# Hybrid encoder trunk on one core: the backward direction's products on off-diagonal quarters, PSUM banks in pairs, a residual subtracted by matmul

## The chip, the cores and the metric

One core of a Trainium2 chip. The metric is the time of one execution in microseconds (us); of several runs the median. The engines are TensorE (PE; its weight loads are listed as PEld), VectorE (DVE), ScalarE (ACT), GpSimd (POOL) and SyncE (SP, which issues the DMAs here).

## The reference

Two layers over 256 positions of width 2048. Each: RMS norm, one input projection, two head groups, gates, one output projection, residual. Group A is a delta-rule recurrence (RWKV-7) with 16 heads of 64, run forward and backward with own decays and rates, the two directions summed. Group B is windowed attention with 16 heads, 4 key heads and a sink. Cut to the recurrence:

```python
def step(S, inp):
    r_t, w_t, k_t, v_t, kk_t, a_t = inp
    s_kk = jnp.einsum('bhvk,bhk->bhv', S, kk_t)
    S = (S * w_t[:, :, None, :]
         - s_kk[..., None] * (a_t * kk_t)[:, :, None, :]
         + v_t[..., None] * k_t[:, :, None, :])
    return S, jnp.einsum('bhvk,bhk->bhv', S, r_t)
...
for d, rev in enumerate((False, True)):
    ...
    y = y + wkv_scan(rh, heads(decay), kd, vh, kk, heads(a), rev)
```

## The kernel before

**Projections.** Each tile of 128 output columns is 16 steps over the contraction (`gemm`), each step three matmuls of 128x128 weights against 256 positions: weights and activations are split into a high and a low part, and high*high, low*high and high*low are summed (L269, L270, L271). ScalarE rounds a streamed weight tile to `hi` (L211), VectorE subtracts to get `lo` (L212). `Stream` holds all projection steps in one line.

**Order of the work.** TensorE's order is the order in which the code is written; the other engines' order is set by a scheduler. `window` goes through 14 slots; in each it lets the generators of the recurrence and the attention take their next step and then runs 4 or 5 projection steps. TensorE has one queue, so a matmul that waits holds up the projections written behind it. The tables STAGE_P, STAGE_I, STAGE_B and ATT say in which slots a generator takes a step.

**The recurrence** works on pairs of heads `p` (8 in each layer; head `h` of the pair is partitions 64h to 64h+63), two directions `d`, and four chunks of 64 positions, in three stages that run one or two windows apart:

- `scan_p` prepares: low-rank decay and rate products into `pz` and `pa` (`low_rank`), decay sums, scaled keys.
- `scan_i` builds per chunk the 64x64 matrices `GE` (L711, L718), transposes (`pt`, copied by L748 and L753), and inverts a triangular matrix by doubling over six LEVELS: `pq` (L791), copied to QF by ScalarE, then two halves of `pd` (L802, L804), written into TC and TT under masks (L805, L806). One step of refinement follows (`pf`, FN, `pn`) and gives VF.
- `scan_b` walks the chunks: RH (L837), the product with VF (L851), the state (L861), scaled by VectorE into the next chunk's operand (L863), and the output `py` (L846, L868). Its last step is `pyt` (L885).

In doubling and recurrence each product is 64 by 64, with head h's operand on partitions 64h and its result on partitions 64h: a diagonal quarter of the array, for both directions.

**PSUM.** Eight banks: two for projections, one each for `py` and `pcc` (all other results of the recurrence), and a ring of four single banks, `ps_w`, which `wbank` hands out in turn. A bank is written again when the readers of its last tile are done.

**Attention** runs late in each layer: `scores` (L917), `flip` (eight transposes L944 into two banks, copied by L947), `values` (L956).

Of the kernel before, what the change touches and what calls it, by code (L numbers as in the profile page):

```python
# [46 lines left out]
STAGE_B = (list(range(1, 14)), [2])  # L47
# [81 lines left out]
def hybrid_trunk_kernel(ctx, tc, xT, wi, wv, wo, par, fing, dup, iup, sink, pos, cst, out):  # L129
# [165 lines left out]
    EYE = cp.tile([128, 64], F16, name="EYE")  # L295
# [6 lines left out]
    def setup():  # L302
        posi = st("t1", [T], I32, bufs=3)
        SY.dma_start(out=posi, in_=pos.to_broadcast([128, T]))
        SY.dma_start(out=FG, in_=fing)
        SY.dma_start(out=SK, in_=sink.to_broadcast([128, DEPTH * 16]))
        cin = st("mv", [C_N - C_KEEP], bufs=3)
        SY.dma_start(out=cin, in_=cst[:, C_KEEP:C_N])
        for l in range(DEPTH):
            s = DP[:, l, 0:NSH]  # L310
            V.tensor_tensor(s, PR[:, l, P_MU0 : P_MU0 + NSH], PR[:, l, P_MU1 : P_MU1 + NSH], op=ALU.add)
            V.tensor_scalar(s, s, -1.0, 1.0, op0=ALU.mult, op1=ALU.add)
            h = DP[:, l, NSH : NSH + 8]
# [36 lines left out]
        V.tensor_copy(band, cin[:, 0:512])  # L350
        V.tensor_copy(EYE, cin[:, 512 + 64 * NL : 576 + 64 * NL])
        yield
# [248 lines left out]
    def layer(l):  # L601
# [24 lines left out]
        def scan_p(p, t):  # L626
# [5 lines left out]
            pz = wbank("pz")  # L632
# [4 lines left out]
            pa = wbank("pa")  # L637
# [65 lines left out]
        def scan_i(p, t):  # L703
            VV, BK, MV = t["v"], t["BK"], t["MV"]
            flat = lambda x: x.rearrange("p d c j -> p (d c) j")
            GE = [st(f"ge{h}", [2, NC, 2, 64], bufs=2) for h in range(2)]
            for d in range(2):
                pgs = [wbank("pg") for _ in range(2)]
                for c in range(NC):
                    for h in range(2):  # L710
                        PE.matmul(  # L711
                            pgs[h][:, c * 128 : (c + 1) * 128],
# [4 lines left out]
                for h in range(2):  # L717
                    V.tensor_tensor(  # L718
                        GE[h][:, d].rearrange("p c s j -> p c (s j)"),
                        pgs[h].rearrange("p (c x) -> p c x", c=NC),  # L720
                        gm[d].unsqueeze(1).to_broadcast([128, NC, 128]),
                        op=ALU.mult,
                    )
# [6 lines left out]
            pts = [wbank("pt") for _ in range(2)]  # L730
# [16 lines left out]
            for h in range(2):  # L747
                A.activation(BT[:, h].rearrange("p d i j -> p (d i j)"), pts[h][:, 0:384], AF.Copy)  # L748
# [21 lines left out]

            TC = st("tv", [2, NC, 64], F16)
# [5 lines left out]
            dch = [(d, c, h) for d in range(2) for c in range(NC) for h in range(2)]  # L777
            hq = lambda x, d, c, h: x[half[h], d, c, :]
            quarter = lambda x, d, c, h: x[half[h], d * T + c * 64 : d * T + (c + 1) * 64]
            for li, b in enumerate(LEVELS):  # L780
# [5 lines left out]
                sub = lambda x, d, c, h, o: pick(x, half[h], d * T + c * 64 + o, [2 * b, 32 // b], [1, b])  # L786
                narrow = lambda x, d, c, h: x[half[h], d * 128 + c * 32 : d * 128 + (c + 1) * 32]
                flat4 = lambda x: x[:, 0:256].rearrange("p (d n b) -> p d n b", d=2, b=b)
                pq = wbank("pq")
                for d, c, h in dch:  # L790
                    PE.matmul(narrow(pq, d, c, h), hq(AB, d, c, h), sub(TC, d, c, h, d * b), start=True, stop=True)  # L791
                if li == 0:
                    V.copy_predicated(t_sub(TC), t_mask, flat4(pq))
                    V.copy_predicated(v_sub(TT), v_mask, v_sub(AB))
                    yield
                    continue

                A.activation(t_sub(QF), flat4(pq), AF.Copy)  # L798
                yield
                pd = wbank("pd")  # L800
                for d, c, h in dch:
                    PE.matmul(narrow(pd, d, c, h), hq(TT, d, c, h), sub(QF, d, c, h, d * b), start=True, stop=True)  # L802
                for d, c, h in dch:
                    PE.matmul(narrow(pd[:, T : 2 * T], d, c, h), hq(QF, d, c, h), sub(TT, d, c, h, (1 - d) * b), start=True, stop=True)  # L804
                V.copy_predicated(t_sub(TC), t_mask, flat4(pd))  # L805
                V.copy_predicated(v_sub(TT), v_mask, flat4(pd[:, T : 2 * T]))  # L806
                yield
            pf = wbank("pf")
            for d, c, h in dch:
                PE.matmul(quarter(pf, d, c, h), hq(AB, d, c, h), hq(TC, d, c, h), start=True, stop=False, skip_group_check=True)  # L810
                PE.matmul(quarter(pf, d, c, h), hq(AL, d, c, h), hq(TC, d, c, h), start=False, stop=True, skip_group_check=True)
            FN = st("q16", [2, NC, 64], F16)
            V.tensor_tensor(FN.rearrange("p d c j -> p (d c j)"), pf, TC.rearrange("p d c j -> p (d c j)"), op=ALU.subtract)
            yield
            pn = wbank("pn")
            for d, c, h in dch:
                PE.matmul(quarter(pn, d, c, h), hq(FN, d, c, h), hq(TT, d, c, h), start=True, stop=True)
# [7 lines left out]
        def scan_b(p, t):  # L825
            GE, MV, BT, SUV, PC, bv = (t[n] for n in ("GE", "MV", "BT", "SUV", "PC", "bv"))

            py = ps_c.tile([128, NC, 64], F32, tag="y", name="py")
            A.activation(py, MSK, AF.Copy, scale=0.0)
            for i in range(NC):  # L830
                ci = [order[d][i] for d in range(2)]
                pc = ps_c.tile([128, 3, 2, 64], F32, tag="c", name="pcc")
                for d in range(2):
                    for h in range(2):

                        r = half[1 - h] if i == 0 else every
                        PE.matmul(pc[half[h], 0, d, :], GE[h][r, d, ci[d], 0, :], SUV[r, d, ci[d], h, :], start=True, stop=True)  # L837
                RH = st("rh", [2, 64], bufs=2)
                A.activation(RH, pc[:, 0], AF.Copy)  # L839
                yield  # L840

                here = lambda h, i=i: pick(SUV, half[h], i * 128 + h * 64, [NC * 128 + (NC - 1 - 2 * i) * 128, 2], [1, 64])
                if i > 0:
                    for d in range(2):
                        for h in range(2):
                            PE.matmul(  # L846
                                py[half[h], ci[d], :], MV[half[h], d, ci[d], 1, :], SUV[half[h], d, ci[d], h, :], start=False, stop=False, skip_group_check=True
                            )
                for d in range(2):
                    for h in range(2):  # L850
                        PE.matmul(pc[half[h], 1, d, :], t["VF"][half[h], d, cs(ci[d])], RH[half[h], d, :], start=True, stop=True)  # L851
                if 0 < i < NC - 1:
                    for h in range(2):
                        PE.matmul(pc[half[h], 2], ident[half[h], half[h]], here(h), start=True, stop=False, skip_group_check=True)  # L854
                for h in range(2):
                    A.activation(here(h), pc[half[h], 1], AF.Copy)  # L856
                yield
                if i < NC - 1:
                    for d in range(2):
                        for h in range(2):  # L860
                            PE.matmul(pc[half[h], 2, d, :], BT[:, h, d, i, :], SUV[:, d, ci[d], h, :], start=(i == 0), stop=True, skip_group_check=True)  # L861
                    for h in range(2):
                        V.tensor_tensor(  # L863
                            here(h, i + 1), pc[half[h], 2], pick(PC, half[h], i, [2 * NC - 1 - 2 * i, 2], [0, 64]), op=ALU.mult
                        )
                for d in range(2):
                    for h in range(2):
                        PE.matmul(py[half[h], ci[d], :], GE[h][:, d, ci[d], 1, :], SUV[:, d, ci[d], h, :], start=False, stop=False, skip_group_check=True)  # L868
# [36 lines left out]
        def scores(j):  # L905
# [3 lines left out]
            pss = [wbank("pscr") for _ in range(2)]  # L909
# [196 lines left out]
```

## Time and profile before

| | |
|---|---|
| median of 3 runs | 1246.04 us (1242.67 to 1246.2) |
| profiled execution, its own time | 1244.23 us |
| its span, first to last instruction | 1242.4 us |
| TensorE busy | 1202.6 us, 97% |
| VectorE busy | 947.5 us, 76% |
| ScalarE busy | 735.6 us, 59% |
| TensorE's granted clock, mean | 0.993 |
| DMA | 134 GB/s mean |

How to read it: "busy" counts an engine while an instruction of it runs. A row of a group names line, engine, operation, output and inputs, shape, count, then busy time, mean of one in ns, and the idle time before with what ended it. "64*64" in a matmul's row is the part of the array in use, rows by columns. A float32 matmul of the code that is not of the rounded kind leaves two records, an fp16 one leaves one. Timeline rows give start and duration in us and join records that follow each other.

### The profile page before, as it was taken

What the parts mean: (1) busy time and instruction counts of PE and PEld (TensorE: products, weight loads), DVE (VectorE), ACT (ScalarE), POOL (GpSimd) and SP (SyncE); (2) the same over time, 40 slices, a digit from 0 to 9 for tenths busy, and PEclk for the clock granted to TensorE, in tenths of its full rate; (3) what the DMA queues carried; (4) which work ended last, traced back from release to release, by engine and by line L of the source; (5) the groups of instructions that cost most, each with busy time, mean ns of one, the idle gap of its engine ahead of it and who ended that gap; (6) DMA issues with size and microseconds to landing.
All of it is one profiled execution on the core that took longest, in us unless ns stands there. A gap on an engine that the chain in (4) does not pass through costs nothing.

```text
span 1242.4 us, 37905 instructions
## 1 busy us (share of the span) xinstructions
PE 1202.6 (97%) x16044; PEld 1113.0 (90%) x16044; DVE 947.5 (76%) x2113; ACT 735.6 (59%) x1838; POOL 18.7 (2%) x23
## 2 busy tenths in 40 slices
PE   7989999999999999999998999999999999999996
PEld 6978999999998889899998888999999989899996
DVE  6988878888886668866666888888887766786654
ACT  6655665666565466655555655665766555675553
POOL 0000000000000000000000000000000000000000
PEclk9999999999999999999999999999999999999998
DMA  6543333223322334367653433323222333435653
GB/s 244 164 141 121 100 103 109 104 93 110 104 97 94 125 112 144 123 225 240 209 186 140 144 104 110 104 99 110 104 93 104 102 112 126 139 131 175 211 191 119
DMA packets 60410, 166.68 MB, mean 134 GB/s; under 512 B 7729, under 2 KB 22737, under 8 KB 60241
## 3 DMA queue, kind: packets, MB, share of 16 engines
q1 hardware_dynamic: 60240, 164.27, 39.0%
q8 instruction: 125, 2.05, 0.6%
q14 instruction: 45, 0.36, 0.1%
HBM read 157.43 MB, written 4.19 MB: 130 GB/s over the span
## 4 chain that ended last, share of the span: by engine, by line
PE 57%; issue 15%; DVE 12%; ACT 9%; DMA 4%; SPq 1%; POOL 0%; DVEq 0%; POOLq 0%; ACTq 0%
PE pm L269 15%; PE pm L271 12%; PE pm L270 12%; DVE lo L212 3%; DMA g<-dup 3%; PE pg L711 2%; ACT hi L211 2%; PE pq L791 2%; PE pd L802 2%; DVE lw L654 1%; PE pcc L837 1%; ACT suv L753 1%; PE pd L804 1%; DMA rrot<-u 1%; PE py L846 1%
## 5 line engine op out<-in xcount | busy, mean ns | idle before, releaser
L269 PE MATMUL pm<-XH,hi 128*128 128x256 f32 x1664 | 496.9, 299 | 10.8 <-ACT XH L174 6.0
L271 PE MATMUL pm<-XH,lo 128*128 128x256 f32 x1664 | 471.3, 283 | 11.5 <-DVE lo L212 11.5
L270 PE MATMUL pm<-XL,hi 128*128 128x256 f32 x1664 | 469.1, 282 | 0.0
L211 ACT ACTIVATE hi<-raw 128x512 fp32r<-128x512 f32 x560 | 327.9, 624 | 205.6 <-PE pm L270 160.4
L212 DVE TENSOR_TENSOR lo<-raw,hi 128x512 fp32r<-128x512 f32 x560 | 369.8, 687 | 99.3 <-ACT hi L211 90.6
L269 PEld LDWEIGHTS pm<-XH,hi 128*128 128x128 f32 x1664 | 315.1, 189 | 36.7 <-issue 13.0
L271 PEld LDWEIGHTS pm<-XH,lo 128*128 128x128 f32 x1664 | 315.7, 190 | 17.0 <-DVE lo L212 16.9
L270 PEld LDWEIGHTS pm<-XL,hi 128*128 128x128 f32 x1664 | 315.8, 190 | 0.7 <-DVE XL L175 0.7
L269 PE MATMUL pm<-MH,hi 128*128 128x256 f32 x512 | 143.9, 281 | 0.7 <-ACT hi L211 0.7
L271 PE MATMUL pm<-MH,lo 128*128 128x256 f32 x512 | 143.7, 281 | 0.4 <-DVE lo L212 0.4
L270 PE MATMUL pm<-ML,hi 128*128 128x256 f32 x512 | 143.6, 280 | 0.0
L269 PEld LDWEIGHTS pm<-MH,hi 128*128 128x128 f32 x512 | 96.4, 188 | 1.7 <-ACT hi L211 1.0
L271 PEld LDWEIGHTS pm<-MH,lo 128*128 128x128 f32 x512 | 96.4, 188 | 0.6 <-DVE lo L212 0.6
L270 PEld LDWEIGHTS pm<-ML,hi 128*128 128x128 f32 x512 | 96.4, 188 | 0.0
L839 ACT ACTIVATE rh<-pcc 128x128 f32<-128x128 f32 x64 | 17.5, 273 | 66.9 <-PE pcc L837 66.5
L856 ACT ACTIVATE suv<-pcc 64x128 f32<-64x128 f32 x128 | 34.1, 266 | 20.9 <-PE pcc L854 19.9
L932 ACT ACTIVATE mv<-mv,mx 128x257 f32<-128x257 f32 x64 | 31.9, 503 | 19.5 <-DVE mx L929 19.4
L791 PE MATMUL pq<-tv,AB 64*64 64x32 f16 x1536 | 40.5, 181 | 1.6 <-DVE tv L805 1.1
L718 DVE TENSOR_TENSOR ge<-pg,C 128x512 f32<-128x512 f32 x64 | 41.2, 683 | 0.7 <-PE pg L711 0.7
L791 PEld LDWEIGHTS <-AB 64*64 64x64 f16 x1536 | 33.7, 109 | 7.7 <-issue 1.1
L711 PE MATMUL pg<-mv,bk 64*128 64x128 f32 x512 | 37.2, 285 | 0.0
L798 ACT ACTIVATE QF<-pq 128x256 f16<-128x256 f32 x80 | 30.8, 385 | 9.5 <-PE pq L791 6.6
(230 smaller groups left out, 1866.7 us busy)
## 6 DMA issues: line engine op xcount, KB each, us to landing
raw<-wi SPq DMA_DIRECT2D x207, 512.0 KB
raw<-wo SPq DMA_DIRECT2D x64, 512.0 KB
raw<-wv SPq DMA_DIRECT2D x8, 512.0 KB
rrot<-u SPq DMA_DIRECT2D x80, 32.0 KB
vg<-xT SPq DMA_DIRECT2D x16, 128.0 KB
xd<-vg SPq DMA_DIRECT2D x16, 128.0 KB
vg<-xd SPq DMA_DIRECT2D x16, 128.0 KB
g<-dup SPq DMA_DIRECT2D x16, 97.0 KB
```

The source lines that it names most:

```text
L211: A.activation(hi[:, q], raw[:, q], AF.Copy)
L212: V.tensor_tensor(lo[:, q], raw[:, q], hi[:, q].bitcast(F32), op=ALU.subtract)
L269: PE.matmul(pm, wh, rh[:, kk, :], start=(kk == 0), stop=False)
L270: PE.matmul(pm, wh, rl[:, kk, :], start=False, stop=False)
L271: PE.matmul(pm, wl, rh[:, kk, :], start=False, stop=(kk == 15))
L711: PE.matmul(pgs[h][:, c * 128 : (c + 1) * 128], BK[half[h], d, c, 1 - h : 3 - h, :].rearrange("p s j -> p (s j)"), MV[half[h], d, c].rearr ...
L718: V.tensor_tensor(GE[h][:, d].rearrange("p c s j -> p c (s j)"), pgs[h].rearrange("p (c x) -> p c x", c=NC), gm[d].unsqueeze(1).to_broadca ...
L791: PE.matmul(narrow(pq, d, c, h), hq(AB, d, c, h), sub(TC, d, c, h, d * b), start=True, stop=True)
L798: A.activation(t_sub(QF), flat4(pq), AF.Copy)
L802: PE.matmul(narrow(pd, d, c, h), hq(TT, d, c, h), sub(QF, d, c, h, d * b), start=True, stop=True)
L856: A.activation(here(h), pc[half[h], 1], AF.Copy)
L932: A.activation(Sc[:, h, q, 0:257], Sc[:, h, q, 0:257], AF.Exp, scale=0.125, bias=mx[:, q : q + 1], accum_out=den[:, q : q + 1])
```

## The change

**Quarters.** In doubling and in the recurrence, the backward direction's products (d = 1) of one half read partitions of head h and write those of the other head, h^1: `half[h ^ d]`. So four products, two heads by two directions, use the four quarters. QF, TT and VF of the backward direction stand on swapped halves, which the second half of `pd` and `pn` swap back: those stay on the diagonal. TT's first level, a plain masked copy of AB before, needs the swapped copy of AB for the backward direction; two matmuls with EYE make it, and a second masked copy takes it in.

**Banks in pairs.** `ps_w` becomes two buffers of two banks (`wpair`), since the two directions write different banks. `wbank` hands out the first bank of a pair. `pz` and `pa` share one pair `pza`; the two banks of `pg`, of `pt`, of the attention's `pscr` and `ppt` become one pair each. GE of both heads becomes one tile, filled by one VectorE instruction per direction, and `pt` is copied by one ScalarE instruction. `py` and the state share a tile `pyc` of two banks; the product with VF goes to a pair `pu`. The clearing of `py` by ScalarE falls away, a start flag takes its place. The step with `pyt` moves from slot 2 to 3.

**Residual.** FN was `pf` minus TC on VectorE. Now a product with NEYE (minus the identity) is added in `pf`, and ScalarE copies the sum.

```diff
-STAGE_B = (list(range(1, 14)), [2])
+STAGE_B = (list(range(1, 14)), [3])
...
-    ps_w = pool("ps_w", 4, space=PSUM)
+    ps_w = pool("ps_w", 2, space=PSUM)
+    def wpair(name):
+        return ps_w.tile([128, 2, 512], F32, tag="w", name=name)
     def wbank(name):
-        return ps_w.tile([128, 512], F32, tag="w", name=name)
+        return wpair(name)[:, 0]
...
-            pz = wbank("pz")
+            pza = wpair("pza")
+            pz, pa = pza[:, 0], pza[:, 1]
...
             A.activation(LW, pz, AF.Tanh, scale=0.5)
-            pa = wbank("pa")
...
-            dch = [(d, c, h) for d in range(2) for c in range(NC) for h in range(2)]
+            dch = [(d, c, h) for c in range(NC) for d in range(2) for h in range(2)]
+            hx = lambda x, d, c, h: x[half[h ^ d], d, c, :]
...
-                    PE.matmul(narrow(pq, d, c, h), hq(AB, d, c, h), sub(TC, d, c, h, d * b), start=True, stop=True)
+                    PE.matmul(narrow(pq[:, d], h ^ d, c), hq(AB, d, c, h), sub(TC, h, d, c, d * b), start=True, stop=True)
...
-                    PE.matmul(narrow(pd, d, c, h), hq(TT, d, c, h), sub(QF, d, c, h, d * b), start=True, stop=True)
+                    PE.matmul(narrow(pd[:, d], h, c), hx(TT, d, c, h), sub(QF, h ^ d, d, c, d * b), start=True, stop=True)
...
-                    PE.matmul(narrow(pd[:, T : 2 * T], d, c, h), hq(QF, d, c, h), sub(TT, d, c, h, (1 - d) * b), start=True, stop=True)
+                    PE.matmul(narrow(pd[:, 0, 128 + d * 128 :], h ^ d, c), hx(QF, d, c, h), sub(TT, h ^ d, d, c, (1 - d) * b), start=True, stop=True)
...
+                    PE.matmul(
+                        pf[half[h ^ d], d, 0:T], NEYE[half[h]], TC[half[h], d].rearrange("p c j -> p (c j)"), start=True, stop=False, skip_group_check=True
+                    )
...
-            V.tensor_tensor(FN.rearrange("p d c j -> p (d c j)"), pf, TC.rearrange("p d c j -> p (d c j)"), op=ALU.subtract)
+            A.activation(FN.rearrange("p d c j -> p d (c j)"), pf[:, :, 0:T], AF.Copy)
...
-            py = ps_c.tile([128, NC, 64], F32, tag="y", name="py")
-            A.activation(py, MSK, AF.Copy, scale=0.0)
+            pyc = ps_c.tile([128, 2, 512], F32, tag="yc", name="pyc")
+            pS = pyc[:, 0, 0:128].rearrange("p (d j) -> p d j", d=2)
+            py = pyc[:, 1, 0:256].rearrange("p (c j) -> p c j", j=64)
...
-                        PE.matmul(pc[half[h], 1, d, :], t["VF"][half[h], d, cs(ci[d])], RH[half[h], d, :], start=True, stop=True)
+                        x = half[h ^ d]
+                        PE.matmul(pu[half[h], d, 0:64], t["VF"][x, d, cs(ci[d])], RH[x, d, :], start=True, stop=True)
...
-                            here(h, i + 1), pc[half[h], 2], pick(PC, half[h], i, [2 * NC - 1 - 2 * i, 2], [0, 64]), op=ALU.mult
+                            here(h, i + 1), pS[half[h]], pick(PC, half[h], i, [2 * NC - 1 - 2 * i, 2], [0, 64]), op=ALU.mult
...
+            pp2 = wpair("ppt")
             for h in range(2):
-                ppt = wbank("ppt")
+                ppt = pp2[:, h]
```

Three places in TensorE's order, with the engines that a row waits for in brackets (Activation is ScalarE, DVE is VectorE).

TensorE, a step of `scan_b` in a steady window: state (L861, later L891), then output (L868, later L898). Before:

```order
L270 MATMUL pm<-XL,hi 128x256
L271 MATMUL pm<-XH,lo 128x256
L861 MATMUL pcc<-suv,bt 64x64 [waits Activation_49]
L861 MATMUL pcc<-suv,bt 64x64 x3
L868 MATMUL py<-suv,ge_3544 64x64
L868 MATMUL py<-suv,ge_3545 64x64
```

The output followed the state with no wait of its own. After:

```order
L275 MATMUL pm<-XH,lo 128x256
L891 MATMUL pyc<-suv,bt 64x64 [waits Activation_49] x2
L891 MATMUL pyc<-suv,bt 64x64 x2
L898 MATMUL pyc<-suv,ge 64x64 [waits DVE_49]
L898 MATMUL pyc<-suv,ge 64x64 x3
```

Now the output's first matmul waits for VectorE; the count it waits for is that of the second L893 (L863 before), the product that reads this step's state.

TensorE, the low-rank products of `scan_p`. Before:

```order
L618 MATMUL pz<-acc,duh 128x256
L619 MATMUL pz<-TW,du 128x256
L617 MATMUL pa<-XA,iuh 128x256 [waits Activation_49]
L618 MATMUL pa<-rrot,iuh 128x256
L619 MATMUL pa<-XA,iu 128x256
```

The wait was for the bank's last reader, a copy of `pt` from two slots ahead (L753). After:

```order
L623 MATMUL pza<-acc,duh 128x256
L624 MATMUL pza<-TW,du 128x256
L622 MATMUL pza<-XA,iuh 128x256 [waits Activation_49]
L623 MATMUL pza<-rrot,iuh 128x256
L624 MATMUL pza<-XA,iu 128x256
```

The row looks alike, but the count is now that of L642 (L636 before), the tanh that reads the first half, which the matmul just ahead has only finished.

TensorE, the transposes of `flip` in the attention. Before:

```order
L271 MATMUL pm<-XH,lo 128x256
L944 MATMUL ppt<-C,mv 128x128 [waits PE_49]
L944 MATMUL ppt<-C,mv 128x128 x3
L944 MATMUL ppt<-C,mv 128x128 [waits DVE_49]
L944 MATMUL ppt<-C,mv 128x128 x3
```

The second head's wait was for the older reader of another bank. After:

```order
L979 MATMUL ppt<-C,mv 128x128 [waits DVE_49]
L979 MATMUL ppt<-C,mv 128x128 x3
L979 MATMUL ppt<-C,mv 128x128 [waits Activation_49]
L979 MATMUL ppt<-C,mv 128x128 x3
L273 MATMUL pm<-XH,hi 128x256
```

The second head's transposes wait for L982 (L947 before), the copy of the first head's.

More of the change, by code (lines that the diff above doesn't have):

```diff
@@ L294, in hybrid_trunk_kernel @@
     MSK = cp.tile([128, NC, 64], F16, name="MSK")
-    EYE = cp.tile([128, 64], F16, name="EYE")
+    EYE, NEYE = (cp.tile([128, 64], F16, name=n) for n in ("EYE", "NEYE"))
     band = cp.tile([128, 512], BF16, name="band")
@@ L351, in setup @@
         V.tensor_copy(EYE, cin[:, 512 + 64 * NL : 576 + 64 * NL])
+        V.tensor_scalar(NEYE, EYE, -1.0, None, op0=ALU.mult)
         yield
@@ L728, in scan_i @@
             yield
-            pts = [wbank("pt") for _ in range(2)]
+            pt2 = wpair("pt")
+            pts = [pt2[:, h] for h in range(2)]
             for b in range(2):
@@ L792, in scan_i @@
[L792 to L794 removed]
+                sub = lambda x, r, d, c, o: pick(x, half[r], d * T + c * 64 + o, [2 * b, 32 // b], [1, b])
+                narrow = lambda o, r, c: o[half[r], c * 32 : (c + 1) * 32]
+                flat4 = lambda x: x.rearrange("p d (n b) -> p d n b", b=b)
+                pq = wpair("pq")
+                if li == 0:
+                    for d, c, h in dch:
+                        PE.matmul(narrow(pq[:, 0, d * 128 :], h, c), hq(AB, d, c, h), sub(TC, h, d, c, d * b), start=True, stop=True)
+                    for h in range(2):
+                        PE.matmul(pq[half[1 - h], 1, 0:T], EYE[half[h]], AB[half[h], 1].rearrange("p c j -> p (c j)"), start=True, stop=True)
+                    V.copy_predicated(t_sub(TC), t_mask, flat4(pq[:, 0, 0:256].rearrange("p (d x) -> p d x", d=2)))
+                    one = lambda x, o: pick(x, every, o, [2 * b, 128 // b], [1, b])
+                    V.copy_predicated(one(TT, b), v_mask[:, 0], one(AB, b))
+                    V.copy_predicated(one(TT, T), v_mask[:, 1], one(pq[:, 1], 0))
@@ L867, in scan_b @@
                     for h in range(2):
-                        PE.matmul(py[half[h], ci[d], :], GE[h][:, d, ci[d], 1, :], SUV[:, d, ci[d], h, :], start=False, stop=False, skip_group_check=True)
+                        PE.matmul(
+                            py[half[h], ci[d], :], GE[h][:, d, ci[d], 1, :], SUV[:, d, ci[d], h, :],
+                            start=(i == 0 and d == 0), stop=(i >= NC // 2), skip_group_check=True,
+                        )
                 if i < NC - 1:
```

72 lines of the change are left out of this document (37 added, 35 removed).

## The prediction

> **What bounds the kernel now.** I read the page's first two parts, then the table by stretches of the span, then who waited for whom, then the groups by line, and last the timeline of one steady stretch.
>
> ```profile
> span 1242.4 us, 37905 instructions
> PE 1202.6 (97%) x16044; PEld 1113.0 (90%) x16044; DVE 947.5 (76%) x2113; ACT 735.6 (59%) x1838; POOL 18.7 (2%) x23
> 750.00:850.00 100.00, 99.89 (x1727) 90.36 (x1724) 86.09 (x180) 62.21 (x165) 2.01 (x2) 1.00 0.30 101
> PE pm L271 <- DVE lo L212: 11.9, 18, 1.6
> PE pcc L837 <- DVE suv L863: 1.7, 2, 1.4
> ```
>
> In the steady stretch TensorE is busy for 99.89 of 100 us at full clock, VectorE for 86, ScalarE for 62. Over the whole span TensorE waited 11.9 us for its largest releaser and 1.7 us for the recurrence. So TensorE is the bound. Work taken from it shortens the span, and a wait put into its queue, which holds the projections too, lengthens it almost one for one.
>
> **What the quarters bring.** The bursts that the change spreads, by groups and in the timeline (start us, us, engine, line, operation; "x16" are sixteen records that follow each other):
>
> ```profile
> L791 PE MATMUL pq<-tv,AB 64*64 64x32 f16 x1536 | 40.5, 181 | 1.6 <-DVE tv L805 1.1
> L802 PE MATMUL pd<-QF,tt 64*64 64x32 f16 x1280 | 33.4, 181 | 0.0
> L804 PE MATMUL pd<-tt,QF 64*64 64x32 f16 x1280 | 32.4, 179 | 0.0
> L851 PE MATMUL pcc<-rh,vf 64*64 64x64 f32 x512 | 25.9, 220 | 0.0
> L810 PE MATMUL pf<-tv,AB 64*64 64x64 f16 x256 | 10.6, 195 | 0.6 <-DVE tv L805 0.6
> ```
>
> ```profile
> 258.79 0.68 PE L885 MATMUL pyt<-C,ysq 64*64 64x64 f32 x16
> 259.31 0.33 PE L851 MATMUL pcc<-rh,vf 64*64 64x64 f32 x5
> 259.43 0.27 PE L734 MATMUL pt<-C,vg 64*64 64x64 f32 x1
> 259.43 0.22 PE L851 MATMUL pcc<-rh,vf 64*64 64x64 f32 x1
> 259.44 0.27 PE L734 MATMUL pt<-C,vg 64*64 64x64 f32 x1
> 259.48 0.22 PE L851 MATMUL pcc<-rh,vf 64*64 64x64 f32 x2
> 259.54 0.40 PE L734 MATMUL pt<-C,vg 64*64 64x64 f32 x14
> 262.61 0.42 PE L791 MATMUL pq<-tv,AB 64*64 64x32 f16 x16
> 266.36 0.28 PE L619 MATMUL pz<-TW,du 97*128 97x256 f32 x1
> 266.47 0.28 PE L617 MATMUL pa<-XA,iuh 96*128 96x256 f32 x1
> ```
>
> L885 and L851 use the two diagonal quarters, L734 already all four. Without the last record's own 0.22 us, L885 starts one matmul per (0.68-0.22)/15 = 31 ns and L734 one per (0.40-0.22)/13 = 14 ns, in the same shape: four quarters run at twice the pace of two. The fp16 burst L791 takes (0.42-0.18)/15 = 16 ns per matmul on two quarters, so 8 on four. Per burst of 16 that saves 0.128 us.
>
> - Levels 2 to 6, pq: 5 bursts for 16 head pairs, 80 x 0.128 = 10.2 us. Level 1 stays on the diagonal; its two new products with EYE use the other quarters, 0 to 0.22 us each head pair; I take 0, since L734 ran beside L851.
> - pd, first half (L802): 80 x 0.128 = 10.2 us. The second half (L804) lands on diagonal quarters for both directions: 0. pn likewise: 0.
> - pf: 32 matmuls at 8 ns less, 0.256 us, against four new 256-column products with NEYE, 0.11 us side by side and 0.44 us in a row (the pace of the two 256-column rows at 266.36 and 266.47). I take side by side: 16 x 0.146 = 2.3 us.
> - The products of the recurrence with VF (L851): 8 records at 31 ns, half of it saved, 0.124 us x 64 = 7.9 us; the first RH of each head pair likewise, 16 x 0.124 = 2.0 us.
>
> Sum 32.6 us at most. The lower end is a start pace that can't go under L734's 14 ns: then the fp16 bursts gain 2 ns a matmul, 160 bursts x 16 x 2 ns = 5.1 us, and the sum is 15 us. I take 32.6, because the rows at 259.43 and 259.44 show three starts within 10 ns.
>
> One rule of the Trainium skill speaks against this, in "TensorE: Matmul & The Clock Gate", under "What overlaps and what doesn't": matmuls start and end strictly in program order. The new order within a burst meets diagonal quarters as A, B, B, A, and by that rule L804's 80 bursts and pn's 16 would, by an estimate, lose some 4 us. The trace disagrees: two L734 records start at 259.43 and 259.44, ahead of the last two of L851 at 259.48, which stand before them in the program.
>
> **What the shared tiles cost.** Two things that had tiles of their own now share one, and the program then makes TensorE wait for the reader of the one before it writes the other. The trace shows what such a wait within a burst does:
>
> ```profile
> 390.18 0.28 PE L734 MATMUL pt<-C,vg 64*64 64x64 f32 x2
> 390.89 0.45 PE L734 MATMUL pt<-C,vg 64*64 64x64 f32 x14 [0.43 <-DVE ge L718]
> 391.80 0.39 PE L269 MATMUL pm<-XH,hi 128*128 128x256 f32 x1
> ```
>
> The third record starts 0.71 us after the first; the projections behind it come only after the burst. There are four such places; these rows, and the two at 266.36 and 266.47 above, size them:
>
> ```profile
> 131.70 0.40 PE L868 MATMUL py<-suv,ge 128*64 128x64 f32 x8
> 131.99 0.59 DVE L863 TENSOR_TENSOR suv<-pcc,pc 64x128 f32<-64x128 f32 x2 [1.24 <-PE pcc L861]
> 262.28 0.40 PE L868 MATMUL py<-suv,ge 128*64 128x64 f32 x8
> 263.34 0.58 DVE L863 TENSOR_TENSOR suv<-pcc,pc 64x128 f32<-64x128 f32 x2
> 267.53 0.60 ACT L636 ACTIVATE lw<-pz 128x512 f32<-128x512 f32 x1
> 272.27 0.40 PE L868 MATMUL py<-suv,ge 128*64 128x64 f32 x8
> 273.50 0.69 DVE L212 TENSOR_TENSOR lo<-raw,hi 128x512 fp32r<-128x512 f32 x1
> 274.11 0.58 DVE L863 TENSOR_TENSOR suv<-pcc,pc 64x128 f32<-64x128 f32 x2
> 281.72 0.40 PE L868 MATMUL py<-suv,ge 128*64 128x64 f32 x8
> 282.79 0.58 DVE L863 TENSOR_TENSOR suv<-pcc,pc 64x128 f32<-64x128 f32 x2
> 264.15 0.77 ACT L753 ACTIVATE suv<-pt 64x256 f32<-64x256 f32 x2
> 472.69 1.04 PE L944 MATMUL ppt<-C,mv 128*128 128x128 f32 x8
> 474.48 0.58 ACT L947 ACTIVATE pp<-ppt 128x512 f32<-128x512 f32 x1
> ```
>
> (a) py behind the state, 48 times. Today L868 follows L861 at once, and VectorE's two products L863 come when they come. In the changed program the first py product waits for the second of them. Floor: at 131.99 VectorE stood idle for L861 and still ended at 132.58, 0.88 us after L868 began. Ceiling: VectorE as late as in the steady stretch, 263.92-262.28 = 1.64, 274.69-272.27 = 2.42 and 283.37-281.72 = 1.65 us for the three steps. I take the floor for the first and third, since VectorE catches up while TensorE stands. The second hangs on a chain of VectorE's own: from L636's end (268.13) to L863's end it took 6.56 us, and the new order puts one more L212 (0.69 us) ahead, 7.25. TensorE needs 272.27-266.47 = 5.80 us from pa to L868, less 0.25 saved: 5.55. So 1.7 us. Twelve head pairs at 0.88+1.7+0.88 = 41.5 us; the last two of each layer have no preparation beside them, 4 x 2.64 = 10.6. Sum 52.1 us.
>
> (b) pa behind L636, 16 times: pz and pa share a pair. Floor: last pz matmul 266.36+0.28, L636's 0.60, against pa's start at 266.47: 0.77 us. Ceiling: L636 as late as now, 268.13-266.47 = 1.66 us. I take 1.2, the middle, since ScalarE keeps the copies of RH and QF ahead of it: 19.2 us.
>
> (c) pq of level 1 behind the copies of pt, 12 times: with two buffers it takes the pair that pt leaves. Today L753 ends at 264.92, 2.31 us after pq began. Now pyt's burst (258.79 to 259.31, 0.52 us) stands between, and the pause of (a), 0.88 us: 0 to 0.9 us remain. I take 0.2, since two ScalarE copies that went ahead now go behind: 2.4 us.
>
> (d) The second head's transposes of the attention behind the first head's copy, 16 times. L944's eight start at 0.11 us each, so the second four are due at 473.13. Floor: 473.02+0.27+0.58 = 473.87, 0.74 us. Ceiling: the copy's end at 475.06, 1.93 us. I take 1.1, nearer the floor, since ScalarE is the least loaded of the three: 17.6 us.
>
> **The rest.** L718's two products over 512 columns become one over both banks, FN's subtraction goes from VectorE to ScalarE, pt's two copies become one, the clearing of py falls away, TT of level 1 is copied in two parts: neither engine is the bound, and the next reader stands a slot away. If that cover were gone, FN would cost its one pass of 0.6 us (as L636) x 16 = 10 us. pyt one slot later is waited for by nobody. Attention's other tiles are released before they are taken again. No DMA and no row of SP or POOL moves.
>
> **Sum.** -32.6 + 52.1 + 19.2 + 2.4 + 17.6 = +58.7 us. The profiled execution took 1244.2 us, so 1302.9; the median of the runs shown lies 1.8 us higher: 1305. With every wait at its floor the costs are 42.2+12.3+0+11.8 = 66.3 us and the time is 1280; with every wait at its ceiling 91.4+26.6+10.8+30.9 = 159.7 us, 1373.
>
> **The rivals.**
>
> - Faster, 1213 us. The waits cost nothing, because the releaser is done when TensorE comes, or TensorE runs the projections past the waiting row, as it ran L734 past L851. The gain decides when the 92 waits average under 32.6/92 = 0.35 us. Against it: the two L863 alone take 0.58, and at 390.89 TensorE did not run past.
> - The queues do not catch up: up to 1373, all ceilings. For it: VectorE's 86%. Against it: each pause of TensorE lowers that share.
> - The quarters don't do what they should, start pace 14 ns: gain 15 instead of 32.6, 1322 us. It lies within the range.
>
> **Chances.** Waits between floors and ceilings, 1272 to 1350: 0.80, with the 1322 of the weak quarters in it. Ceilings beyond 1350: 0.07. A little above before, 1250 to 1272, some waits below their floors: 0.02. Within 0.3%, which is about what the runs can tell from no change: 0.03. Faster: 0.08. So 0.08, 0.03, 0.89, and the range is 1272 to 1350.
>
> **What would show it.** Right: new rows among TensorE's waits, py on the state's product (48 times, 40 to 60 us with the drain), pza on lw, ppt on pp; TensorE's idle time up from 40 to some 120 us; pq and L819's bursts of 16 lasting 0.30 us instead of 0.42. VectorE's busy share falls under 73%. Wrong: bursts that keep 0.42 us, or py rows that follow the state's rows with no idle time, or a lower granted clock.

## The result, and the profile after

The changed kernel takes 1358.79 us (median of 4 runs, 1355.82 to 1360.66) against 1246.12 us (1242.67 to 1247.05): ratio 1.0907, 95% interval 1.0877 to 1.0938, 112.7 us slower. I had forecast 1305 us, in a range of 1272 to 1350: the sign was right, the size 54 us too small. The profiled execution spans 1354.0 us, 111.6 more than before.

The first lines of the page of after (span; busy time of each engine):

```profile
span 1354.0 us, 38019 instructions
PE 1209.1 (89%) x16140; PEld 1107.6 (82%) x16140; DVE 946.0 (70%) x2082; ACT 742.4 (55%) x1822; POOL 18.9 (1%) x23
```

Span minus busy time was 39.8 us before and is 144.9 us now: TensorE stands 105.1 us longer. Its busy time has not fallen either, though its bursts got shorter. For whom TensorE waits in after (engine, tile and line; releaser; us, times, longest):

```profile
PE pyc L898 <- DVE suv L893: 53.8, 48, 2.9
PE pza L622 <- ACT lw L642: 28.6, 16, 6.5
PE ppt L979 <- ACT pp L982: 17.2, 16, 1.5
PE pq L813 <- DVE tv L806: 7.7, 13, 0.7
PE pm L275 <- DVE lo L216: 7.0, 9, 1.3
PE pm L273 <- ACT hi L215: 3.7, 2, 2.4
PE pq L803 <- ACT suv L759: 1.2, 2, 0.6
```

The first three rows are the forecast's (a), (b) and (d), 99.6 us; before, none of them stood in this list. The fourth is new and was not forecast. The last is (c). (Rows that the changed waits do not concern are left out.) One pause of kind (a), in the timeline of a steady stretch:

```profile
258.89 0.45 PE L891 MATMUL pyc<-suv,bt 128*64 128x64 f32 x8
259.19 0.69 DVE L216 TENSOR_TENSOR lo<-raw,hi 128x512 fp32r<-128x512 f32 x1 [0.73 <-ACT hi L215]
259.80 0.58 DVE L893 TENSOR_TENSOR suv<-pyc,pc 64x128 f32<-64x128 f32 x2
260.44 0.45 PE L898 MATMUL pyc<-suv,ge 128*64 128x64 f32 x8 [1.10 <-DVE suv L893]
```

L891 and L898 use 128 rows of the array, so they are not among the products that moved to other quarters. L898 follows L891 after 1.55 us; before, the distance (L861 to L868) was 0.28 us on average. VectorE was busy with a weight tile (L216) when the state came, then made its two products, and only then could py start.

In the single bursts the quarters do what was forecast. Two more pieces of the timeline of after:

```profile
254.01 0.30 PE L819 MATMUL pd<-QF,tt 64*64 64x32 f16 x16
254.16 0.41 PE L821 MATMUL pd<-tt,QF 64*64 64x32 f16 x16
...
256.28 0.27 PE L881 MATMUL pu<-rh,vf 64*64 64x64 f32 x2
256.32 0.23 PE L873 MATMUL pyc<-suv,mv 64*64 64x64 f32 x2
...
256.45 0.20 PE L813 MATMUL pq<-tv,AB 64*64 64x32 f16 x2
256.50 0.28 PE L884 MATMUL pyc<-suv,C 64*64 64x128 f32 x2
```

L819 on four quarters takes 0.30 us for 16 records (L802 before: 0.42), L821 on two still 0.41. L881 starts ahead of the last of L873, which stands before it in the program; L813 ahead of L884. My reading, which no run isolates, is that such a row is held up only by its own quarter. It holds for rows with no wait for another engine: at 260.44 the wait for VectorE held up all that stood behind it.

**The granted clock.** Its mean fell from 0.993 to 0.973: 76.1 us of after are at half clock, in 16 stretches (the last at the end of the program; the expectations below count 15), against 19.9 us in 3 before. (These times run to the end of the clock's record, 2.0 us behind the last instruction.) Windows of 3.4 us in after (start, end and length; busy us of PE, PEld, DVE, ACT, POOL; granted clock; DMA's share and GB/s):

```profile
61.40:64.80 3.40, 1.42 (x12) 1.21 (x11) 2.12 (x4) 1.47 (x3) 0.00 (x0) 1.00 0.32 74
64.80:68.20 3.40, 0.00 (x0) 0.00 (x0) 0.00 (x0) 0.39 (x2) 0.00 (x0) 0.50 0.81 286
68.20:71.60 3.40, 2.84 (x13) 2.84 (x14) 2.43 (x5) 2.16 (x6) 0.00 (x0) 0.50 0.03 11
71.60:75.00 3.40, 3.40 (x18) 3.40 (x18) 1.35 (x3) 1.65 (x4) 0.00 (x0) 0.50 0.00 0
...
382.25:385.65 3.40, 2.17 (x35) 1.65 (x33) 3.21 (x8) 2.67 (x7) 0.00 (x0) 1.00 0.47 146
385.65:389.07 3.42, 3.35 (x15) 3.36 (x16) 2.38 (x5) 1.68 (x5) 0.00 (x0) 0.50 0.53 167
389.07:392.48 3.41, 3.41 (x72) 3.22 (x70) 3.23 (x8) 2.51 (x8) 0.00 (x0) 1.00 0.00 0
```

After a window in which TensorE worked 1.42 or 2.17 us comes one at half clock. It takes no long standstill: in the second case pauses of together 1.2 us were enough. To price it I took, for all matmuls that started at half clock, the distance to the next start, and subtracted the mean distance of the same pair of lines at full clock (distances of 0.6 us or more left out). That gives 24.7 us in after, 3.3 before: 21.4 us of the 111.6 are the clock's. I use this measure, "the clock's excess", below.

### The profile page after: what moved, and what is told of

It is laid out like the page before. It is cut to its first block, busy times and chain, and to the rows that moved or that the text cites. A ratio compares the mean times of both kernels' runs of the same rounds, so it can differ in the third digit from the quotient of the medians.

```text
span 1354.0 us, 38019 instructions
## 1 busy us (share of the span) xinstructions
PE 1209.1 (89%) x16140; PEld 1107.6 (82%) x16140; DVE 946.0 (70%) x2082; ACT 742.4 (55%) x1822; POOL 18.9 (1%) x23
## 5 line engine op out<-in xcount | busy, mean ns | idle before, releaser
L216 DVE TENSOR_TENSOR lo<-raw,hi 128x512 fp32r<-128x512 f32 x560 | 369.5, 687 | 118.7 <-ACT hi L215 109.0
L273 PEld LDWEIGHTS pm<-XH,hi 128*128 128x128 f32 x1664 | 322.1, 194 | 35.1 <-issue 13.0
L275 PEld LDWEIGHTS pm<-XH,lo 128*128 128x128 f32 x1664 | 322.2, 194 | 8.4 <-DVE lo L216 8.4
L274 PEld LDWEIGHTS pm<-XL,hi 128*128 128x128 f32 x1664 | 322.6, 194 | 0.7 <-DVE XL L179 0.7
L898 PE MATMUL pyc<-suv,ge 128*64 128x64 f32 x512 | 29.0, 234 | 53.8 <-DVE suv L893 53.8
L898 PEld LDWEIGHTS pyc<-suv,ge 128*64 128x64 f32 x512 | 20.1, 136 | 62.5 <-DVE suv L893 60.4
L868 ACT ACTIVATE rh<-pyc 128x128 f32<-128x128 f32 x64 | 17.3, 270 | 85.2 <-PE pyc L866 85.2
L886 ACT ACTIVATE suv<-pu 64x128 f32<-64x128 f32 x128 | 34.3, 268 | 27.9 <-PE pq L813 19.1
L399 DVE TENSOR_TENSOR u<-pm,rb 128x256 f32<-128x256 f32 x52 | 21.2, 410 | 34.4 <-PE pm L275 32.5
L724 DVE TENSOR_TENSOR ge<-pg,C 128x1024 f32<-128x1024 f32 x32 | 39.1, 1221 | 3.6 <-PE pg L718 3.6
L822 DVE CAST_PREDICATED tv<-LV,pd 128x256 f16<-128x256 uint8 x80 | 34.4, 430 | 9.7 <-PE pd L821 9.6
```

The costliest lines, as they stand in the source:

```text
L216: V.tensor_tensor(lo[:, q], raw[:, q], hi[:, q].bitcast(F32), op=ALU.subtract)
L273: PE.matmul(pm, wh, rh[:, kk, :], start=(kk == 0), stop=False)
L274: PE.matmul(pm, wh, rl[:, kk, :], start=False, stop=False)
L275: PE.matmul(pm, wl, rh[:, kk, :], start=False, stop=(kk == 15))
L399: V.tensor_tensor(u, pm, L.norm.rb, op=ALU.mult)
L724: V.tensor_tensor(GEd(d), pg.rearrange("p h (c x) -> p h c x", c=NC), gm[d].unsqueeze(1).unsqueeze(1).to_broadcast([128, 2, NC, 128]), op= ...
```

## The experiments

Theory: each shared tile costs its pause, one for one. Rivals: a pause taken away comes back at the next wait; the clock is a cost of its own.

**e1: py and state in tiles of their own.**

```diff
-            pyc = ps_c.tile([128, 2, 512], F32, tag="yc", name="pyc")
+            pcc = ps_c.tile([128, 512], F32, tag="c", name="pcc")
+            pyt = ps_c.tile([128, 512], F32, tag="y", name="py")
```

The first RH of each pair is then copied in two instructions instead of one.

> The changed kernel, with py and the state in two tiles of one bank each instead of one tile of two banks, so that py's products no longer wait for VectorE's product of the state. Theory (each wait of a shared tile costs its own drain, and nothing takes its place): the 48 pauses at L898, 53.8 us of idle time and 62 us from start to start, go; 1359 - 62 = 1297 us, with 1285 to 1308 as the clock comes back or not. Rival 1 (the wait moves: TensorE only comes sooner to the next product that needs VectorE or ScalarE, RH on suv or pq on tv): over 1330 us, with new rows of 20 us or more among TensorE's waits. Rival 2 (the clock gate: a window of 3.4 us in which TensorE is busy for half or less is followed by one at half clock): half-clock stretches fall from 15 to 8 or fewer, and the gain is 5 to 10 us more than the pauses alone, 1287 to 1292.

Measured: 1291.67 us, 67.1 less. No row of py's wait is left, and the row of L813, 7.7 us in after, has gone with it, so that wait too hangs on the shared tile. Half-clock time is 51 us in 10 stretches, the clock's excess 14.3. But (c), now uncovered, grew from 1.2 to

```profile
PE pq L803 <- ACT suv L759: 11.5, 12, 1.5
```

So 67 us are one tile's sharing with its after-effects: 62.0 us of pauses (taken from start to start, below), 7.7 of L813 and 10.4 of the clock, less 10.3 for (c), would make 69.8. (c) was small only because (a) covered it, as the prediction's working for (c) had it.

**e2: both low-rank products ahead of the tanh.**

```diff
-            LW = st("lw", [2 * T])
-            A.activation(LW, pz, AF.Tanh, scale=0.5)
             for d in range(2):
                 low_rank(pa[...
+            LW = st("lw", [2 * T])
+            A.activation(LW, pz, AF.Tanh, scale=0.5)
```

> The changed kernel, with both low-rank products (pz and pa) written before ScalarE's tanh of the first, so that pa does not wait for it. Theory (a wait costs its own drain): 37 us from start to start go, or 25 if the two long ones of 6.5 us at the layers' starts are ScalarE's lateness and come back at the next product; 1322 to 1334 us. Rival (the wait moves to the next reader of ScalarE's work): 1345 us or more.

Measured: 1343.65 us, only 15.1 less, though the row of pza, 28.6 us, is gone. The waits of e2 say where it went; in after these rows had 53.8, 7.0 and 3.7:

```profile
PE pyc L898 <- DVE suv L893: 58.7, 48, 2.8
PE pm L275 <- DVE lo L216: 10.6, 13, 1.6
PE pm L273 <- ACT hi L215: 6.9, 4, 2.0
```

The other engines had used the pause to catch up. The time lies between the two ranges, 1.4 us short of the rival's, and the rival's reason holds: of 28.6 us of idle time about half comes back, at these rows.

**e3: the flip's eight transposes ahead of both copies** (the loop over the copies is split off).

> The changed kernel, with all eight transposes of the attention's flip before the two copies. Theory: 16 pauses of 1.1 to 1.3 us go, 17 to 21 us; 1338 to 1342 us. Rival (values waits for the copies instead, or VectorE's scores): 1352 or more.

Measured: 1338.27 us, 20.5 less, as expected by the theory.

**e4: all three.**

> The three edits together. Theory (the three waits add up and the quarters' gain of 22 to 33 us remains): 1246 - 22 to 1246 - 33 us, so 1213 to 1224; with some 9 us of new wait at level 1 of the doubling left, 1220 to 1233. TensorE's busy share is back at 96% or more. Rival 1 (part of the waits moves): 1250 to 1300. Rival 2 (the clock gate is a cost of its own, set by windows with TensorE at half busy or less): half-clock stretches are back at 3 to 5, against 15, and the gain over the changed kernel exceeds the sum of the three single edits or of their idle times (53.8 + 28.6 + 17.2 = 99.6 us) by 10 us or more.

Measured: 1247.09 us, ratio to before 1.0007 (0.9996 to 1.0017): the three waits are worth 111.7 us together, the whole loss; alone they gave 67.1 + 15.1 + 20.5 = 102.7. Half-clock time is 26.8 us in 5 stretches. But the quarters' gain is not there, and the time is in no range of the expectation; of the second rival the stretches came, and the gain stands near its mark of 10 us: 9.0 over the sum of the single ones, 12.1 over the idle times. Page and waits of e4:

```profile
PE 1180.6 (95%) x16140; PEld 1088.7 (88%) x16140; DVE 937.3 (75%) x2082; ACT 738.4 (59%) x1838; POOL 19.0 (2%) x23
...
PE pq L803 <- ACT suv L759: 10.0, 11, 1.5
```

TensorE works 22.0 us less than before and stands 23.6 us longer, 10.0 of it in (c); the rest is spread over rows that grew by 3.5 us or less.

**e5: e4, and two of the four copies of pt on VectorE**, against (c).

> The three edits together, and two of the four copies of pt into suv on VectorE instead of ScalarE. With the three waits gone, TensorE's row pq of level 1 waits 10.0 us in 11 times for ScalarE's last copy of pt, term (c) of the prediction, which had been sized at 2.4 us because the pauses of (a) covered it. Theory: that wait is what hides the quarters' gain; it goes, and the time is 1247 - 8 to 1247 - 11, so 1236 to 1239 us, 0.8% under the kernel before. Rival (the wait moves: VectorE, 75% busy, gets later, and TensorE waits for lo or for the state's product instead): 1243 to 1250.

Measured: 1245.28 us, 0.9995 (0.9984 to 1.0006): no change.

```profile
PE 1180.6 (95%) x16140; PEld 1089.9 (88%) x16140; DVE 951.2 (76%) x2114; ACT 729.1 (59%) x1806; POOL 19.0 (2%) x23
...
PE pq L805 <- DVE suv L762: 14.0, 12, 1.7
...
261.17 0.85 DVE L762 COPY suv<-pt 64x256 f32<-64x256 f32 x2 [0.92 <-ACT suv L764]
```

The copies read the two banks of one pair and write one tile, and VectorE's wait for ScalarE's to end (the last row, of the timeline). So TensorE's wait changed engines. The time is in the rival's range, but not for its reason: the wait for lo stayed (11.1 us, 11.4 in e4).

**e6: e5 with all products on the diagonal** (`h ^ d` becomes `h`).

> The kernel of the previous run, with the backward direction's products put back on the diagonal quarters (h ^ d becomes h everywhere; banks, tiles and order unchanged). It prices the quarters alone. Theory by the rows of the three edits together (pq -6.7 us, both halves of pd -4.4, pf -1.9, the recurrence's products with VF and MV -4.4 against before): slower by 15 to 20 us. The prediction's own sum: slower by 32.6. Rival (TensorE's start pace binds and four quarters bring little): slower by 5 or less.

Measured: 1267.67 us, 1.0177 (1.0158 to 1.0196), 22.4 us over e5, between the theory's 15 to 20 and the prediction's 32.6.

```profile
PE 1212.0 (95%) x16140; PEld 1121.1 (88%) x16140; DVE 955.9 (75%) x2114; ACT 729.4 (57%) x1806; POOL 19.0 (1%) x23
```

TensorE's busy time differs by 31.4 us; the spans differ by 25.1, since e5 stands 6.3 us longer. The rest of the change, without quarters and without the three waits (but with e5's copies), costs 21.9 us (e6 against the runs of before beside it, 1245.76): 12.8 are (c), and pq and pf, with the products with EYE and NEYE in them, take 6.0 us more from start to start. So in e5 a gain of 22.4 us and a cost of 21.9 cancel. That they are so nearly equal is chance.

**e7: e5 with the residual subtracted on VectorE** (the backward direction then takes the other half's TC; only the time is read).

> The kernel of the run before last, with the residual's subtraction back on VectorE: no products with NEYE, FN is pf minus TC on VectorE. Theory (four 256-column products side by side cost TensorE 2.1 us in all, and VectorE has slack there): 2 us faster, from 3 faster to no change. Rival (pn then waits for VectorE): 4 to 10 us slower.

Measured: 1250.27 us, 1.0036 (1.0023 to 1.0048), 5.0 us over e5. The rival's time holds, but the wait is at another row than it said (pg, not pn); so in e5 the move to TensorE is worth 5 us:

```profile
PE pg L718 <- DVE ge L724: 8.1, 14, 0.7
```

**e8 and e12: the pause filled.** Four products of the identity with itself into pu's bank (e8), then two into unused columns of the projections' bank (e12):

```diff
+                    if S.cur is not None:
+                        for _ in range(2):
+                            PE.matmul(S.cur[:, T : T + 128], ident, ident, start=True, stop=True, skip_group_check=True)
```

> The changed kernel, with four products of the identity with itself (128x128, float32, into a part of pu's bank that nobody reads) between the state's products and the waiting py, 48 times: TensorE works through most of the pause that it otherwise stands idle in. They add no result. Theory of the clock gate (in the trace of the changed kernel all 19 windows of 3.4 us with TensorE busy for half or less but one are followed by a window at half clock, none of those at 0.67 or more; 15 such stretches, about 16 us of longer projections): half-clock stretches fall to 8 or fewer and the kernel gets faster, by 5 to 12 us, though it does more work: 1347 to 1354 us. Rival (the pauses cost their idle time and nothing else): 1359 to 1364, no change or a little slower, where fillers outlast a pause.

> The changed kernel, with two products of the identity with itself (128x128, float32, 0.37 us each as the earlier run with four of them showed) in the pause between state and py, 48 times, now into a part of the projections' bank that nobody reads, so that no buffer is held longer. They add no result. Theory of the clock gate (a window of 3.4 us with TensorE busy for half or less is followed by one at half clock): they lift the share of windows that hold two pauses; half-clock stretches fall from 15 to 8 or fewer, and the kernel gets faster by 4 to 10 us, 1349 to 1355. Rival (pauses cost only their idle time): 1358 to 1364.

Measured: e8 1373.65 us, outside both ranges. It tells nothing on the clock: pu's buffer was held longer, and a new wait came up,

```profile
PE pyt L920 <- ACT suv L759: 24.8, 12, 2.2
```

e12, whose fillers also disturb the projections' sums: 1350.22 us, 8.6 less than the changed kernel, with work added. That is in the theory's range and below the rival's 1358. Half-clock time fell from 76.1 to 60.6 us, less than expected (11 stretches, not 8); the clock's excess fell by 5.7 us.

**e9 and e10: e4, with three or two of slot 3's projection steps run ahead of level 1 of the doubling.**

> The three edits together, and in slot 3 of a window three of the five projection steps run ahead of level 1 of the doubling instead of behind it, so that TensorE has work while ScalarE copies pt. Theory (the wait for the copies of pt, 10.0 us in 11 times with the three edits alone, is what stands between that kernel and a gain): 1247 - 8 to 1247 - 10, 1237 to 1239 us. Rival (level 2 then comes too soon after level 1, and TensorE waits for VectorE's copy into TC instead): 1243 to 1249.

> As the run before, with two projection steps ahead of level 1 and three behind. Theory: two steps last 0.72 us and the wait was 0.91 us on average, so some 2 us of it stay; 1238 to 1241 us. Rival (the wait for VectorE's copy into TC takes over): 1243 to 1249.

Measured: 1276.54 us (1.0238, 1.0215 to 1.0262) and 1261.39 us (1.0118, 1.0103 to 1.0133). The rival's wait came in both, but the times are far above its 1249 us. (c) is all but gone, and in its place stands, in e9,

```profile
PE pq L816 <- DVE tv L809: 21.3, 16, 1.4
```

Close behind it pza waits for the same copies (3.2 us). TensorE stands 5.4 us longer than in e4, but the profiled span grew by 26.1: the clock's excess rose from 6.4 to 23.4 us (half-clock time from 26.8 to 70.7). No expectation had that.

**e11: the changed kernel, with three projection steps run between state and py; e14: this and e2's edit.**

> The changed kernel, shared tiles and all, with three of the slot's projection steps run between the state's products and the waiting py. The wait stays in the program, the work that the pause keeps from running goes into it. Theory (a pause costs what TensorE has to stand for, not the wait itself): three steps take 1.08 us of the 1.3 us, so 53.8 us of idle time fall to some 12; 1300 to 1315 us, near the kernel with separate tiles (1292). Rival (VectorE gets later by the steps' own demands, and the wait stays as long): over 1330.

> The kernel with the covered pause (1333 us), and both low-rank products written before ScalarE's tanh. There, level 2 of the doubling waits 15.3 us in 14 times for VectorE and pza 29 us in 26 times right behind it, in the same slot: two pauses within one window of 3.4 us, and 108 us at half clock, the most of all kernels, though its idle time is 103 us against 145 of the changed kernel. Theory of the clock gate (each us at half clock adds 0.58 us to TensorE's busy time, as the kernels so far line up): with one of the two pauses gone, half-clock time falls to some 50 us, and the time falls by 29 + 0.58 * 58 = 62 us, to 1265 to 1280. Rival (only idle time counts): by 29 us or less, to 1304 or more.

Measured: e11 1332.76 us, e14 1305.56: both in the range of the rival, not of the theory. Waits of e11, then the busy time in e14:

```profile
PE pza L627 <- ACT lw L647: 26.3, 16, 6.5
PE pq L818 <- DVE tv L811: 15.3, 14, 1.7
PE pyc L904 <- DVE suv L898: 3.9, 5, 1.5
```

```profile
span 1300.9 us, 37994 instructions
PE 1209.3 (93%) x16140; PEld 1101.8 (85%) x16140; DVE 943.8 (73%) x2082; ACT 741.1 (57%) x1822; POOL 19.0 (1%) x23
```

In e11 the wait of (a) is covered, 3.9 us of 53.8 are left, against the rival's reason; yet only 26 us come back: the second row doubled and stands in the same slot as the first, two pauses in one window, and half-clock time is 108 us (excess 33.6), the most of all kernels. With the first row gone, in e14, half-clock time is 50.9 us (excess 16.4), as the theory said; its price was wrong. The span fell by 30.2 us: 11.1 less idle time (102.7 to 91.6) and 19.1 less busy time (1228.4 to 1209.3), of which the clock's excess is 17.2. That is half of the 62 expected: busy time fell by 0.33 us for each us less at half clock, not by the 0.58 of a line through the earlier kernels, and of pza's 26.3 us some 15 came back in other waits. Against the rival's reason, that only idle time counts, stand the 19.1 us of busy time.

**e13: e4, with pyt after level 1 and three projection steps.**

> The three edits together, and in slot 3 the pair's last product pyt comes after level 1 of the doubling and three of the slot's five projection steps, instead of ahead of both. Level 1 then takes the pair of banks that pu left a slot ago, and pyt the one of pt, whose copies are long done. Theory (the wait for the copies of pt was the last that the change brought; it goes, and VectorE's copy into TC, with pyt's work no longer ahead of it, comes early): waits of 10 us go, half-clock time falls a little, 1232 to 1238 us, 0.7 to 1.1% under the kernel before. Rival (the wait moves to pza, which takes the pair of pyt): 1243 to 1250.

Measured: 1249.48 us, 1.003 (1.0019 to 1.004). The rival holds: (c) is gone, and waits of 13.2 us are in its place (the last row stood at 2.0 in e4).

```profile
PE pza L626 <- ACT t L929: 5.1, 10, 0.5
PE pq L817 <- DVE tt L827: 5.1, 10, 0.6
PE pq L817 <- DVE tv L826: 3.0, 6, 0.9
```

No version beat the kernel before by more than the measurement can tell. TensorE's work still counts (31.4 us more of it in e6 lengthen the span by 25.1), but part of what is cut from it comes back as waits for VectorE and ScalarE. Whether shorter chains through these two would set the gain free, no run here shows.

## Why the prediction was right or wrong

**The bound and the signs, right.** TensorE's pauses lengthened the span; taking away the three that were forecast takes away the whole loss (e4), with the after-effects that hang on them. The new rows, the bursts of 0.30 us and VectorE's share (70%) came as named; idle time is 144.9 us instead of some 120. The rival of weak quarters fell with the bursts, the faster one with L898's row. The rival whose queues do not catch up has the time (up to 1373) but not the mechanism: in the twelve steady head pairs (a) sums to 43.3 us, near my 41.5 and far from the ceilings' 68.5.

**The quarters, right in the burst, too high in the sum.** I had forecast 32.6 us net of the new products with EYE and NEYE. The 31.4 us between e6 and e5 come close by luck: in e6 these products stand on the diagonal and cost 6.0 us that the kernel before has not. Against before, e4 works 22.0 us less, about 25 without the clock's excess (6.4 against 3.3). So the term was some 7 us too high in work; of the 22.4 us of time that e6 shows, the 6.0 too only make good what the new products would cost. That matmuls need not keep the program's order shows in the rows at 256.28 to 256.50, against the rule cited in the prediction.

**(a), right in steady windows, 10 us too small in all:** 52.1 us forecast with the drain. From L891's first start to L898's first it is 75.5 us in all, against 13.5 before, so 62.0 (53.8 of them idle, in 48 waits); 67.1 when undone. Eight of the ten us are in the last two pairs of each layer, 18.6 us where I had 10.6, all floors:

```profile
440.33 0.45 PE L891 MATMUL pyc<-suv,bt 128*64 128x64 f32 x8
441.18 0.42 DVE L495 TENSOR_TENSOR u<-u,TW 128x256 f32<-128x256 f32 x1 [1.92 <-DMA rrot<-u]
...
442.80 0.58 DVE L893 TENSOR_TENSOR suv<-pyc,pc 64x128 f32<-64x128 f32 x2
443.44 0.52 PE L898 MATMUL pyc<-suv,ge 128*64 128x64 f32 x8 [2.66 <-DVE suv L893]
```

No preparation of a later pair stands beside these, as I had said, but preparation of the attention does: L495 and the rows behind it stand ahead of L893 in VectorE's queue, and L495 has waited for a DMA. So it is in all four long pauses of these pairs (those at 440, 474, 1113 and 1136 us).

**(d), 3 us too small:** 17.6 forecast, 20.8 from start to start (17.2 of them idle), 20.5 when undone. **(c), right in after** (2.4 forecast, 1.2 idle), but 10 to 14 us in e1 and e4 to e7, where (a) is gone. It is the largest wait there that before did not have; yet taking it away (e9, e10, e13) brought no gain, since other waits came.

**(b), the step that failed most.** 16 x 1.2 = 19.2 us forecast. From start to start pza takes 61.8 us against 24.4 for pz and pa, 37.4 more, 28.6 of it idle; the first pairs of the two layers alone take 14.3 more, where my 1.2 each made 2.4. I had sized it from one steady pair (row at 266.47). The trace of before held most of the rest, at the first pair of each layer:

```profile
60.41 0.28 PE L619 MATMUL pz<-TW,du 97*128 97x256 f32 x1
60.53 0.29 PE L617 MATMUL pa<-XA,iuh 96*128 96x256 f32 x1
...
64.72 0.42 ACT L436 ACTIVATE duh<-g 97x256 fp32r<-97x256 f32 x1 [3.97 <-DMA g<-dup]
65.05 0.58 ACT L636 ACTIVATE lw<-pz 128x512 f32<-128x512 f32 x1
```

L436, which rounds weights of the next pair, stands ahead of L636 in ScalarE's queue and waits for a DMA. L636 ended 5.1 us after pa had begun; nobody waited for it. In the second layer it was 6.5. The same distance, taken for all 16 pairs, sums to 32.4 us. After the change the same queue holds up TensorE:

```profile
62.54 0.28 PE L624 MATMUL pza<-TW,du 97*128 97x256 f32 x1
67.81 0.42 ACT L441 ACTIVATE duh<-g 97x256 fp32r<-97x256 f32 x1 [4.94 <-DMA g<-dup]
68.13 0.58 ACT L642 ACTIVATE lw<-pza 128x512 f32<-128x512 f32 x1
68.76 0.58 PE L622 MATMUL pza<-XA,iuh 96*128 96x256 f32 x1 [5.94 <-ACT lw L642]
```

In the steady windows pa starts 1.33 us after the row ahead of it, against 0.12 before: 1.2 us more, as I had it.

**The clock, no term at all.** The prediction named a lower granted clock as a sign that it was wrong, and put no price on it: 21.4 us. Of (b)'s long pauses, the one at 62.5 us was followed by 10.2 us at half clock.

**Not foreseen:** L813's wait for VectorE's copy of level 1 (L806), 7.7 us, gone with the shared tile of (a) (e1). **FN, costed at nothing:** that move is a gain of 5 us in e5 (e7); in the changed kernel itself it was not measured.

So the mechanism was right, and the sum failed in its sizes: at (b), 18 us too small, at the clock, which it left out, 21, at L806, 8, and at the quarters, some 7 too much gain; (a) and (d) add 10 and 3. That is more than the 53 us by which the span missed. The terms overlap, since rows at half clock are longer, and the projections' own waits for lo and hi fell from 16.7 to 10.7 us. The range's end at 1350 had no room for the clock.

## What to carry to other kernels

Two things in one tile are one for the program's waits: put a writer and the reader of its neighbour into one tile, and the writer waits. Size such a wait at every place where it occurs, the first and last of a layer too, not at one steady place, and look at what stands ahead of the releaser in its in-order queue. When the busiest engine's work is cut, ask which chain sets the pace next: in six kernels here (e2, e5, e9, e10, e11, e13) a wait that was taken away came back, in part or whole, at the next reader.

## What the runs showed of the hardware

Half clock follows a poorly filled window. I cut the traces of the 16 kernels into the windows of 3.41 us at whose borders the clock changed, and took TensorE's busy share in each at full clock:

| busy share of the window | windows | followed by half clock |
|---|---|---|
| under 0.45 | 78 | 78 |
| 0.45 to 0.55 | 97 | 59 |
| 0.55 to 0.70 | 257 | 35 |
| 0.70 and more | 5326 | 0 |

The Trainium skill, "TensorE: Matmul & The Clock Gate", under "What's actually happening", has the same window and puts the half rate after at least one idle window; here a window about half full was often enough (59 of 97). A kernel with TensorE 95% busy (e9) spent 70.7 us at half clock; the pauses of its largest group of waits were 1.4 us or shorter.
